# A hybrid decoder step: two DeltaNet heads beside each other, and a lane of its own for the last attention pair

## The chip, the cores and the metric

The kernel runs on one NeuronCore of a Trainium2 chip. The core has engines that run side by side, each with its own in-order instruction stream: TensorE (PE, matrix products; its weight loads are shown as PEld), VectorE (DVE), ScalarE (ACT), GpSimd (POOL) and SyncE (SP, which here issues the transfers). The metric is the device time of one execution in microseconds. The kernel before was timed in three runs.

## The reference

The reference is one inference step of a two-layer decoder trunk. A prompt of 2048 tokens with 16 learned tokens ahead of it, and 8 decode sequences of one token each, pass through both layers. Width is 1024, everything is float32.

Layer 0 makes one projection of the normed input and feeds two kinds of heads with it. Eight attention heads (two key and value heads) look at a window of 128 positions. Four gated DeltaNet heads with keys and values of 128 go through a short convolution and then, chunk by chunk, through the delta rule. For each head and chunk:

```python
a_mat = where(strict, (kbeta @ k.T) * decay, 0) + eye
u, w  = triangular_solve(a_mat, [v * beta, kbeta * exp(gc)])
# over the chunks, S carried from one to the next
v_new = u - w @ S
o     = q_dec @ S + qk @ v_new
S     = S * g_last + k_dec.T @ v_new
```

Both results are gated, put side by side and projected out (`w_out_ab`), and added to the input. Layer 1 is linear attention with a data-dependent decay (GLA), four heads with keys of 128 and values of 256, also in chunks, with its own gate and output projection. A last norm makes `y`. The states, the window caches and the last rows of the convolution are outputs too.

## The kernel before, in words

The prompt is cut into 4 groups of 512 tokens, worked through one after the other; group 0 also carries the 16 learned and the 8 decode tokens, so its tiles are 536 columns wide and its projections run in two halves of 268. Activations lie with the channels on the partitions, 8 tiles of 128 channels. Every float32 operand of a large projection is split into a high and a low part; a projection is three products (high by high, high by low, low by high), which appear in the profile as `pp<-t,wh` and `pp<-t,wl` at L110, the line of the helper `MM`. PSUM is split into 4 banks for projections (`pp`) and 4 for everything else (`pc`). In group 0 the weights are split on ACT (`wh<-raw`, L365) and DVE (`wl<-raw`, L113) and written back to memory as parts; later groups load the parts (`wh<-wd`, `wl<-wd`). The weights pass through 8 tiles (`NW`), two for each projection.

A group goes through these stages: `ab_head` (keys, then the convolution of DeltaNet head 0), `ab_rest` (the other three convolutions `c1` to `c3` and the four attention pairs `s0` to `s3`, in the order of the list `ORDER`), `ab_out` (the output projection in two parts, the first over those of the 8 mixed outputs that come first in `OUT_AB`), `c_main` (GLA) and `c_out`. The head of the next group (`ab_head`) stands inside `c_out` of the group before.

Projections are the bulk work and are emitted by `bulk`. Everything else is a generator that yields a planned latency and its planned TensorE time. `spawn` puts a generator into a lane; a lane runs one generator at a time, and the next starts no earlier than the time at which the last one ended. A clock `Clock.pe` counts planned TensorE time; between two pieces of a projection, `bulk` lets every stream step whose time has come:

```python
while streams:
    s = min(streams, key=lambda q: q[0])
    if s[0] > Clock.pe:
        break
    step(s)
```

The tile framework then orders the instructions of each engine from what was emitted and its dependencies.

Tiles are counted by hand. `take` waits for room in bulk code and meanwhile drives the streams on (`advance`); `take_in` does so inside a stream by yielding. `T` is the pool of wide work tiles (52, of which 47 may be taken), `BQ` a pool of four larger tiles: a DeltaNet head needs two (its convolved queries and keys, and its products), a GLA head three (values, queries and keys, output).

A DeltaNet head (`dn_head`) is a chain of 34 steps: transposed keys (L1466), decays, products, the inverse of the triangular matrix by doubling from 32x32 blocks (tiles `inv`, products `pc<-inv,t` and `pc<-inv,inv`), transposed values and queries (L1583, L1591), then for each of 4 chunks three steps with the state, and last a norm and the transposes of the output (L1637). All heads run in the lane `dn`. In group 0 the learned tokens are a chunk of their own in the lane `dnx` and the decode tokens a stream in the lane `smp`.

An attention pair (`swa_pair`) works on one head of each key and value group: scores (products `pc<-kh,t`), softmax, transposes (L1015) and values (`pc<-t,va`), for 4 blocks, and then splits its output with the last subtraction on GpSimd (`store_m`). All pairs run in the lane `swa`. The last pair of `ORDER`, u = 3, has a form of its own with shorter steps. In the GLA stage a head (`gla_head`) multiplies masked products (`AMK`), values (`VH`), scaled keys and the states (`Tg`, `SM`), and its output `On` is transposed at L1812.

Of the kernel before, what the change touches and what calls it, by code (L numbers as in the profile page):

```python
# [21 lines left out]
META = 16  # L22
EX = SMP + META
NT, NT_FREE = 52, 5
NW = 8
AHEAD = 8
W_AHEAD = 1
RS_AT = 5

ORDER = "c1 s0 c2 s1 c3 s2 s3".split()  # L30

# [38 lines left out]
def kernel(ctx: ExitStack, tc: tile.TileContext, ins, outs):  # L70
# [12 lines left out]
    def nm(s):  # L83
        cnt[0] += 1
        return f"{s}_{cnt[0]}"
# [9 lines left out]
        return ft(dt)  # L95

    def t512(shape=(128, 128), dt=F32):
        return wk.tile(list(shape), dt, tag="t512", bufs=4, name=nm("t5"))

    def sm(shape=(128, 32), dt=F32):  # L100
        return wk.tile(list(shape), dt, tag="sm", bufs=20, name=nm("sm"))

    def cb(shape=(128, 512)):
        return pc.tile(list(shape), F32, tag="pc", name=nm("pc"))
# [287 lines left out]
    def step(s):  # L392
        try:
            lat, pe = next(s[1])
            s[0] += lat
            Clock.pe += pe
        except StopIteration:
            s[2] = False
            streams.remove(s)
            lanes[s[3]].pop(0)  # L400
            if lanes[s[3]]:
                n = lanes[s[3]][0]
                n[0] = max(n[0], s[0])
                streams.append(n)

    def bulk(gen, hooks=()):

        for i, c in enumerate(gen):
# [3 lines left out]
            while streams:  # L412
# [2 lines left out]
                    break  # L415
                step(s)

    def join(ss):
        while any(s[2] for s in ss):
            advance()  # L420


    live = {"BQ": 0, "T": 0}
    caps = {"BQ": 4, "T": NT - NT_FREE}

    def room(tag, n=1):
        return live[tag] + n <= caps[tag]
# [15 lines left out]
        live[tag] -= n  # L443

    def until(cond):
        while not cond():
            yield 0.5, 0.0

    def take_in(tag, n=1):
        yield from until(lambda: room(tag, n))  # L450
# [213 lines left out]
    def new_group(g):  # L664
        q = Grp()
        q.g = g
        q.C = CMAX if g == 0 else 512
        q.off = EX if g == 0 else 0
        q.halves = [(0, q.C // 2), (q.C // 2, q.C // 2)] if g == 0 else [(0, 512)]
        q.x0 = 0 if g == 0 else EX + 512 * g  # L670
        q.wins = [(b, q.off + 128 * b) for b in range(4)]
        q.seq0 = SMP if g == 0 else 0
        q.s0 = 1 if g == 0 else 0
        q.nscan = 4 + q.s0
        q.layer = "AB"
        q.M = [[None] * 8, [None] * 8]
        q.can_m = False
        q.dn = []
        q.sw = []
        return q  # L680

# [211 lines left out]
    def ab_conv(q, h):  # L893
        g = q.g
        take("BQ", 2)
        CQ = wk.tile([128, 2, CMAX - SMP], F32, tag="BQ", bufs=4, name=nm("CQ"))
        take("T", 2)
        CV = ft(shape=(128, CMAX - SMP))
        G_, vdone, done = [], [], []

        first, got = [], []

        def meta():
            yield from take_in("T")
            got.append(1)
            yield from dn_head(q, h, CQ, CV, 0, 1, 32, 0, G_, SMP, META, vdone, done, first)

        def chunks():
            if g == 0:
                yield from until(lambda: got)  # L910
            else:
                first.append(1)
            yield from take_in("T", 2)
            yield from dn_head(q, h, CQ, CV, META if g == 0 else 0, 4, 128, q.s0, G_, q.off, 128, vdone, done, first)
            give("BQ")
            give("T")
        for j in range(3):
            ct = 3 * h + j
            Tt = ft()

            def w(i):
                return PV[:, P_CW + 4 * ct + i:P_CW + 4 * ct + i + 1]

            def ev_c(ps, c0, n):

                m = n - q.seq0
                if g == 0:
                    A.copy(XS[:, ct, :], ps[:, 0:SMP])
                    R = ps[:, SMP - 3:n]
                    V.memset(R[:, 0:3], 0.0)  # L930
                else:
                    R = ft()
# [12 lines left out]
            if j == 1:  # L945
                if g == 0:
                    q.dn.append(spawn(meta(), "dnx", 0.5, tag=h))
                s = spawn(chunks(), "dn", LAT["dn_spawn"], tag=h)
                q.dn.append(s)
        vdone.append(1)  # L950
        G_.append(ft())
        bulk(ab_proj(q, 21 + h, gate(q, G_[0], 4 + h)))
        done.append(1)
        if g == 0:
            q.dn.append(spawn(dn_sample(q, h), "smp", tag=h))

    def ab_swa(q, u):
        g, off = q.g, q.off
        take("T", 3)
        QS = [ft(F32R, (128, 512)) for _ in range(2)]  # L960

        def ev_q(ps, c0, n):
            s = 0
            if g == 0:
                for kv in range(2):
                    A.activation(QX[:, 4 * kv + u, :], ps[64 * kv:64 * kv + 64, 0:EX], AF.Copy, scale=0.125)
                s = EX
            m = n - s
            for kv in range(2):
                r = slice(64 * kv, 64 * kv + 64)  # L970
                o = slice(64 - 64 * kv, 128 - 64 * kv)
                A.activation(QS[kv][r, 0:m], ps[r, s:n], AF.Copy, scale=0.125)
                STT(QS[kv][o, 0:m], ps[r, s:n], 0.125, QS[kv][r, 0:m].bitcast(F32), mul, sub)
        bulk(ab_proj(q, 1 + u, ev_q))
        gx = []
        if g == 0 and len(q.sw) == 3:
            q.xs = [spawn(swa_extra(q, gx), "sx", LAT["sx_0"])]
        Gt = ft()
        bulk(ab_proj(q, 5 + u, gate(q, Gt, u)))
        gx.append(1)  # L980
        return spawn(swa_pair(q, u, QS, Gt), "swa", LAT["sw_spawn"])

    def swa_pair(q, u, QS, Gt):
        g, off = q.g, q.off
# [141 lines left out]
    def c_v(q, h):  # L1126
        g, s0 = q.g, q.s0
        take("BQ")
        VH = wk.tile([128, 4, 256], F32, tag="BQ", bufs=4, name=nm("VH"))
        if h == 0:  # L1130
            gkp = cb()
            gkx = cb() if g == 0 else None
# [31 lines left out]
    def c_logs(q):  # L1164

        C = q.C
        yield from take_in("T", 4)
        yield from take_in("BQ", 2)
        q.mn, Bs = [], []
        for p in range(2):  # L1170
            B = wk.tile([128, 2, CMAX], F32, tag="BQ", bufs=4, name=nm("Bc"))
            for h in (2 * p, 2 * p + 1):
                mn = ft()
                bg = PV[:, P_BGK + h:P_BGK + h + 1]
                for (c0, n) in q.halves:
                    ps = cb()
                    MM(ps[:, :n], WU[:, 128 * h:128 * h + 128], GS[:, c0:c0 + n])
                    A.activation(B[:, h % 2, c0:c0 + n], ps[:, :n], AF.Abs, bias=bg)
                    TS(mn[:, c0:c0 + n], ps[:, :n], bg, 0.0, add, amin)
                q.mn.append(mn)  # L1180
                yield LAT["dec_1"], 0.25
            A.activation(B[:, :, :C], B[:, :, :C], AF.Exp, scale=-1.0)
            Bs.append(B)
# [71 lines left out]
    def c_head(q, h, nxt):  # L1255
# [8 lines left out]
        join([q.dec])  # L1264
        E = q.E
        take("BQ", 2)
        QKt = wk.tile([128, 2, CMAX], F32, tag="BQ", bufs=4, name=nm("QKt"))
        for j in range(2):
            def ev_m(ps, c0, n):
                TT(QKt[:, j, c0:c0 + n], ps, E[j][:, c0:c0 + n], mul)  # L1270
# [165 lines left out]
    def dn_head(q, h, CQ, CV, q0, nch, L, s0, G_, mc0, nv, vdone, done, first):  # L1436
# [47 lines left out]
            A.activation(DT[R_, c, 0:L], Rp[R_, c, 0:L], AF.Exp, bias=SC["ng"][R_, s0 + c, h:h + 1])  # L1484
        yield LAT["dn_R"], 0.45 * pe
        if L == 128:
            BQ = wk.tile([128, 4, 2, 128], F32, tag="BQ", bufs=4, name=nm("BQ"))
        else:
            BQ = ftt((128, 1, 64)).rearrange("p c (x l) -> p c x l", x=2)
        for c0 in range(0, nch, 2):  # L1490
# [18 lines left out]


        yield LAT["dn_at"], 0.45 * pe
        tc4 = lambda: wk.tile([128, 4, 32], F32, tag="inv", bufs=6, name=nm("inv"))

        P1, Y, X = tc4(), tc4(), tc4()
        for a in range(nb):
# [60 lines left out]
            A.copy(YF[0:64, :, 64:128], pi[0:64, 1])  # L1576
            yield 0.0, 0.4

        while not vdone:
            yield 0.5, 0.0  # L1580
        vT = cb((128, 4, 128))
        for c in range(nch):
            T.transpose(vT[R_, c], blk(2, c), ident)  # L1583
# [46 lines left out]
        on = O  # L1630
        TT(on[R_, 0:nch], O[R_, 0:nch], bc(st2[R_, 3, 0:nch], 128), mul)
        yield LAT["dn_n"], 0.0
        while not (done and q.can_m):
            yield 0.5, 0.0
        oT = cb((128, 4, 128))
        for c in range(nch):
            T.transpose(oT[:, c, 0:L], on[R_, c], ident[R_, 0:L])  # L1637
# [129 lines left out]
    def gla_head(qq, h, QKt, VH, ce, Gz, done):  # L1767
# [14 lines left out]
        A.copy(KT, kT)  # L1782
        yield LAT["gl_t"], 1.4
        st = sm((128, 4, 4))
        On = wk.tile([128, 4, 256], F32, tag="BQ", bufs=4, name=nm("On"))
        QS = ft(shape=(128, 4, 128))
        TT(QS, QKt[:, 0, off:off + 512].rearrange("p (c t) -> p c t", c=4), bc(ce[:, s0:s0 + 4], 128), mul)
        for c0 in (0, 2):
# [31 lines left out]

    def gla_sample(q, h, QKt, VS, ea, Gz):
        vrow = rows_of(VS[0:8], 256)
        QZ = wk.tile([128, 72], F32, tag="t512", bufs=4, name=nm("QZ"))
        V.memset(QZ, 0.0)
        V.tensor_copy(QZ.rearrange("p (b x) -> p x b", x=9)[:, 0, :], QKt[:, 0, 0:SMP])
        o = cb()
# [155 lines left out]
```

## Time and profile before

| what | value |
|---|---|
| median of 3 runs | 2223.55 us (2215.16 to 2228.36) |
| profiled execution, its own time | 2217.27 us |
| its span, first to last instruction | 2215.5 us |
| PE busy | 2146.0 us (97%), 17290 matmuls |
| PEld busy | 1805.4 us (81%) |
| DVE busy | 1216.4 us (55%) |
| ACT busy | 833.4 us (38%) |
| POOL busy | 263.1 us (12%) |
| granted TensorE clock, mean | 0.988 |
| moved by DMA | 400.17 MB, mean 181 GB/s |

A row of the timeline gives start, duration, engine, line, operation, output<-input with buffer numbers left out, shapes, count, and in brackets the idle time before it with what ended it. Matmuls are pipelined and their ends are modelled, so the time from one start to the next tells more than a duration. A row of the waits names who waited for whom, the total, the number of times and the longest. A row by stage gives a stretch in microseconds from the start of the span, its length and the busy time of each engine in it, the granted clock as a share of full speed, the busy share of the DMA engines and what they moved.

### The profile page before, as it was taken

How to read it: one execution, taken by the hardware profiler on the slowest of the kernel's cores; microseconds unless marked ns; L12 is line 12 of the kernel's file. 1: busy time of each engine (PE TensorE's matmuls, PEld its weight loads, DVE VectorE, ACT ScalarE, POOL GpSimd, SP SyncE). 2: the span in 40 equal slices, each digit the busy share in tenths (PEclk: the TensorE clock that was granted, in tenths of full speed). 3: DMA queues.
4: the chain of work that ended last, by engine and by line, in shares of the span. 5: the costliest groups of instructions: out<-in, count | busy, mean ns of one | idle time of the engine just before them, and what ended most of it. 6: DMA issues, size and time to landing. Idle time of an engine off the chain costs nothing.

```text
span 2215.5 us, 43744 instructions
## 1 busy us (share of the span) xinstructions
PE 2146.0 (97%) x17290; PEld 1805.4 (81%) x17290; DVE 1216.4 (55%) x3501; ACT 833.4 (38%) x2235; POOL 263.1 (12%) x314
## 2 busy tenths in 40 slices
PE   8889999999999999999999999999999999999997
PEld 7878888888879777788887777778887877778886
DVE  7778876654564566544344466545344466545323
ACT  5445544443352244343232244334333244334222
POOL 0011100021210011002220011002130000001111
PEclk9999999999999999999999999999999999999999
DMA  6643537767767623474555823454554743364444
GB/s 237 206 161 125 194 121 245 249 219 262 254 205 246 241 97 103 136 242 149 177 203 164 275 98 115 143 202 170 177 183 148 243 168 104 102 239 159 164 147 153
DMA packets 162623, 400.17 MB, mean 181 GB/s; under 512 B 22049, under 2 KB 54465, under 8 KB 162385
## 3 DMA queue, kind: packets, MB, share of 16 engines
q1 hardware_dynamic: 162416, 397.37, 52.7%
q8 instruction: 136, 2.23, 0.4%
q14 instruction: 71, 0.57, 0.1%
HBM read 297.19 MB, written 101.70 MB: 180 GB/s over the span
## 4 chain that ended last, share of the span: by engine, by line
PE 70%; DMA 3%; DVE 3%; ACT 2%; issue 2%; POOL 1%; SPq 0%; DVEq 0%; POOLq 0%; ACTq 0%
PE pp L110 53%; PE pc L110 14%; DVE t L116 1%; PE pc L1015 1%; DMA wl<-wd 1%; DMA raw<-in_w_co 1%; DMA t<-in_xT 1%; PE pc L1812 1%; DVE t L113 1%; POOL sm L206 0%; POOL t L113 0%; ACT t L1004 0%; PE pc L1583 0%; PE pc L1466 0%; PE pc L1591 0%
## 5 line engine op out<-in xcount | busy, mean ns | idle before, releaser
L110 PE MATMUL pp<-t,wh 128*128 128x512 f32 (+1 forms) x4528 | 1260.3, 363 | 17.6 <-ACT t L150 7.8
L110 PEld LDWEIGHTS pp<-t,wh 128*128 128x128 f32 x4528 | 783.1, 190 | 127.8 <-issue 17.4
L110 PE MATMUL pp<-t,wl 128*128 128x512 f32 (+1 forms) x2264 | 809.2, 358 | 6.3 <-DMA wl<-wd 5.2
L110 PEld LDWEIGHTS pp<-t,wl 128*128 128x128 f32 x2264 | 429.5, 190 | 67.0 <-DMA wl<-wd 6.5
L113 POOL TENSOR_TENSOR t<-t,t 128x512 fp32r<-128x512 f32 (+3 forms) x128 | 163.6, 1295 | 580.9 <-ACT t L660 345.5
L110 PE MATMUL pp<-wh,t 128*128 128x256 f32 (+1 forms) x1088 | 209.6, 288 | 2.9 <-DVE QKt L113 2.9
L116 DVE SCALAR_TENSOR_TENSOR t<-t,PV,t 128x512 f32<-128x512 f32 (+4 forms) x232 | 172.6, 754 | 55.7 <-ACT t L935 23.2
L110 PEld LDWEIGHTS pp<-wh,t 128*128 128x128 f32 x1088 | 172.7, 191 | 5.0 <-DVE QKt L113 3.1
L116 DVE SCALAR_TENSOR_TENSOR t<-pp,t 128x512 f32<-128x512 f32 (+3 forms) x160 | 92.8, 585 | 128.0 <-PE pp L110 78.5
L206 POOL TENSOR_TENSOR sm<-sm,mh 128x2 f32<-128x2 f32 (+3 forms) x84 | 68.0, 809 | 772.5 <-DVE sm L116 320.1
L110 PE MATMUL pp<-wl,t 128*128 128x256 f32 (+1 forms) x544 | 155.3, 286 | 0.0
L113 DVE TENSOR_TENSOR wl<-raw,wh 128x512 fp32r<-128x512 f32 (+3 forms) x138 | 91.5, 680 | 24.2 <-ACT wh L365 12.8
L110 PEld LDWEIGHTS pp<-wl,t 128*128 128x128 f32 x544 | 103.6, 191 | 0.7
L365 ACT CAST wh<-raw 128x512 fp32r<-128x512 f32 (+2 forms) x122 | 68.2, 587 | 61.2 <-DMA raw<-in_w_c 17.9
L113 DVE TENSOR_TENSOR t<-t,t 128x512 f32<-128x512 f32 (+4 forms) x103 | 62.9, 614 | 42.4 <-ACT t L489 41.2
L1004 ACT ACTIVATE t<-t,sm 128x257 f32<-128x257 f32 x128 | 64.1, 503 | 56.8 <-DVE sm L116 56.6
L113 DVE TENSOR_TENSOR QKt<-pp,t 128x512 f32<-128x512 f32 (+1 forms) x40 | 23.3, 586 | 112.1 <-PE pp L110 106.5
L110 PEld LDWEIGHTS pc<-t,t 128*128 128x128 f32 (+4 forms) x496 | 63.7, 165 | 22.4 <-ACT t L1609 3.8
L110 PE MATMUL pc<-t,t 128*128 128x128 f32 (+5 forms) x496 | 79.4, 270 | 1.7 <-PE pc L110 0.7
L489 ACT ACTIVATE t<-t 128x512 f32<-128x512 f32 (+1 forms) x70 | 44.1, 631 | 96.5 <-DVE t L116 66.7
L113 DVE TENSOR_TENSOR t<-pp,t 128x268 f32<-128x268 f32 (+1 forms) x90 | 44.3, 497 | 49.6 <-PE pp L110 36.0
L1017 ACT COPY t<-pc 128x512 f32<-128x512 f32 x64 | 37.4, 584 | 63.7 <-PE pc L1015 63.3
(334 smaller groups left out, 2788.4 us busy)
## 6 DMA issues: line engine op xcount, KB each, us to landing
wh<-wd SPq DMA_DIRECT2D x157, 512.0 KB, 3.7
wl<-wd SPq DMA_DIRECT2D x157, 512.0 KB, 4.6
wd<-wh SPq DMA_DIRECT2D x55, 512.0 KB, 3.5
wd<-wl SPq DMA_DIRECT2D x55, 512.0 KB, 5.1
t<-in_xT SPq DMA_DIRECT2D x72, 256.0 KB, 4.9
raw<-in_w_ab SPq DMA_DIRECT2D x25, 512.0 KB, 5.2
raw<-in_w_c SPq DMA_DIRECT2D x16, 512.0 KB, 4.7
out_yp<-t SPq DMA_DIRECT2D x32, 256.0 KB, 2.9
```

The lines of the kernel that those rows point to most:

```text
L110: T.matmul(out, lhsT, rhs, start=start, stop=stop)
L113: return (eng or V).tensor_tensor(out, a, b, op=op)
L116: V.scalar_tensor_tensor(out, a, s, b, op0=op0, op1=op1)
L206: G.tensor_tensor(out, x, mh[0:x.shape[0]].to_broadcast(list(x.shape)), op=ALU.pow)
L365: last[0] = A.copy(hi[:, c], raw[:, c])
L489: A.activation(sq[:, :q.C], x, AF.Square)
L1004: A.activation(S_[:, kv], S_[:, kv], AF.Exp, bias=st[:, 2 + kv:3 + kv], accum_out=st[:, 4 + kv:5 + kv])
L1015: T.transpose(pt[:, kv, x], S_[:, kv, 128 * x:128 * x + 128], ident)
L1017: A.copy(PT, pt)
L1812: T.transpose(oT[:, c], On[:, c, 128 * j:128 * j + 128], ident)
```

## The change

`ab_conv` no longer puts a head's chunk stream into the lane `dn`. It makes the entry by hand, with a time before which it may not start, and appends it to a list of the group. With head 0 it spawns one stream `together` in the lane `dn`, which works through that list. At most `DN_RUN` = 2 heads run in it, and a head is taken up when the one before has made at least `DN_OFF` = 12 steps. In every round each running head makes one step. The round's latency is the larger of the two, times `PAIR_LAT` = 1.25 when both made a step. `DN_HOLD` adds to a head's earliest time: nothing in group 0, and in the later groups 50 for head 0 and 25 for head 2. A wait inside a stream now yields no latency (`None`), which `step` takes as 0.5 and `together` does not count as a step.

The last attention pair of `ORDER` is spawned into a lane of its own (`swaTrue`), the other three share one (`swaFalse`).

The pools grow: `BQ` from 4 to 6 tiles, also for the GLA stage, `t512` from 4 to 8, `sm` from 20 to 24, `inv` from 6 to 10. The scratch for dynamic DMA is set to 1024.

```diff
+NBQ = 6
...
+PAIR_LAT, DN_OFF, DN_RUN = 1.25, 12, 2
+DN_HOLD = ((0, 0, 0, 0), (50, 0, 25, 0))
...
-        return wk.tile(list(shape), dt, tag="t512", bufs=4, name=nm("t5"))
+        return wk.tile(list(shape), dt, tag="t512", bufs=8, name=nm("t5"))
...
-        return wk.tile(list(shape), dt, tag="sm", bufs=20, name=nm("sm"))
+        return wk.tile(list(shape), dt, tag="sm", bufs=24, name=nm("sm"))
...
-            s[0] += lat
+            s[0] += 0.5 if lat is None else lat
...
+    def together(gens):
+        run, left = [], 4
+        while left:
+            if gens and gens[0][1] <= Clock.pe and len(run) < DN_RUN and (not run or run[-1][1] >= DN_OFF):
+                run.append([gens.pop(0), 0])
+            lat, pe = [], 0.0
+            for a in list(run):
+                r = next(a[0][0], False)
+                if not r:
+                    a[0][2] = False
+                    run.remove(a)
+                    left -= 1
+                elif r[0] is not None:
+                    a[1] += 1
+                    lat.append(r[0])
+                    pe += r[1]
+            yield (max(lat) * (PAIR_LAT if len(lat) > 1 else 1.0) if lat else None), pe
...
-    caps = {"BQ": 4, "T": NT - NT_FREE}
+    caps = {"BQ": NBQ, "T": NT - NT_FREE}
...
     def until(cond):
         while not cond():
-            yield 0.5, 0.0
+            yield None, 0.0
...
-                s = spawn(chunks(), "dn", LAT["dn_spawn"], tag=h)
+                s = [chunks(), Clock.pe + LAT["dn_spawn"] + DN_HOLD[g > 0][h], True, "dn", h]
                 q.dn.append(s)
+                q.pair.append(s)
+                if h == 0:
+                    spawn(together(q.pair), "dn", LAT["dn_spawn"])
...
-        return spawn(swa_pair(q, u, QS, Gt), "swa", LAT["sw_spawn"])
+        return spawn(swa_pair(q, u, QS, Gt), "swa" + str(u == int(ORDER[-1][1])), LAT["sw_spawn"])
...
-        tc4 = lambda: wk.tile([128, 4, 32], F32, tag="inv", bufs=6, name=nm("inv"))
+        tc4 = lambda: wk.tile([128, 4, 32], F32, tag="inv", bufs=10, name=nm("inv"))
...
-    nc = _bacc.Bacc("TRN2", target_bir_lowering=False, num_devices=1)
+    nc = _bacc.Bacc("TRN2", target_bir_lowering=False, num_devices=1, dynamic_dma_scratch_size=1024)
```

The other `BQ` allocations take `bufs=NBQ` as well, and two waits in `dn_head` that yielded 0.5 now use `until`.

More of the change, by code (lines that the diff above doesn't have):

```diff
@@ L678, in new_group @@
         q.dn = []
+        q.pair = []
         q.sw = []
@@ L895, in ab_conv @@
         take("BQ", 2)
-        CQ = wk.tile([128, 2, CMAX - SMP], F32, tag="BQ", bufs=4, name=nm("CQ"))
+        CQ = wk.tile([128, 2, CMAX - SMP], F32, tag="BQ", bufs=NBQ, name=nm("CQ"))
         take("T", 2)
@@ L1128, in c_v @@
         take("BQ")
-        VH = wk.tile([128, 4, 256], F32, tag="BQ", bufs=4, name=nm("VH"))
+        VH = wk.tile([128, 4, 256], F32, tag="BQ", bufs=NBQ, name=nm("VH"))
         if h == 0:
@@ L1170, in c_logs @@
         for p in range(2):
-            B = wk.tile([128, 2, CMAX], F32, tag="BQ", bufs=4, name=nm("Bc"))
+            B = wk.tile([128, 2, CMAX], F32, tag="BQ", bufs=NBQ, name=nm("Bc"))
             for h in (2 * p, 2 * p + 1):
@@ L1266, in c_head @@
         take("BQ", 2)
-        QKt = wk.tile([128, 2, CMAX], F32, tag="BQ", bufs=4, name=nm("QKt"))
+        QKt = wk.tile([128, 2, CMAX], F32, tag="BQ", bufs=NBQ, name=nm("QKt"))
         for j in range(2):
@@ L1486, in dn_head @@
         if L == 128:
-            BQ = wk.tile([128, 4, 2, 128], F32, tag="BQ", bufs=4, name=nm("BQ"))
+            BQ = wk.tile([128, 4, 2, 128], F32, tag="BQ", bufs=NBQ, name=nm("BQ"))
         else:
@@ L1577, in dn_head @@
             yield 0.0, 0.4
-        while not vdone:
-            yield 0.5, 0.0
+        yield from until(lambda: vdone)
         vT = cb((128, 4, 128))
@@ L1632, in dn_head @@
         yield LAT["dn_n"], 0.0
-        while not (done and q.can_m):
-            yield 0.5, 0.0
+        yield from until(lambda: done and q.can_m)
         oT = cb((128, 4, 128))
@@ L1784, in gla_head @@
         st = sm((128, 4, 4))
-        On = wk.tile([128, 4, 256], F32, tag="BQ", bufs=4, name=nm("On"))
+        On = wk.tile([128, 4, 256], F32, tag="BQ", bufs=NBQ, name=nm("On"))
         QS = ft(shape=(128, 4, 128))
@@ L1822, in gla_sample @@
         vrow = rows_of(VS[0:8], 256)
-        QZ = wk.tile([128, 72], F32, tag="t512", bufs=4, name=nm("QZ"))
+        QZ = wk.tile([128, 72], F32, tag="t512", bufs=8, name=nm("QZ"))
         V.memset(QZ, 0.0)
```

## The prediction

> **What bounds the kernel now.** I read the page first, then the busy time by stage, then what TensorE waits for, then the order of time around the places where it waits.
>
> ```profile
> span 2215.5 us, 43744 instructions
> PE 2146.0 (97%) x17290; PEld 1805.4 (81%) x17290; DVE 1216.4 (55%) x3501; ACT 833.4 (38%) x2235; POOL 263.1 (12%) x314
> q1 hardware_dynamic: 162416, 397.37, 52.7%
> ```
>
> TensorE is busy for 2146.0 of 2215.5 us: 69.5 us are idle. The change keeps all 17290 matmuls, so it can win only idle time, the cost of changing between kinds of matmul, and time at a lowered clock. Where these lie (columns: stretch, length, then PE, PEld, DVE, ACT, POOL busy with counts, granted clock, DMA share, GB/s):
>
> ```profile
> 53.30:72.00 18.70, 12.69 (x245) 9.98 (x243) 13.57 (x56) 4.79 (x19) 1.75 (x3) 0.73 0.14 53
> 134.00:147.00 13.00, 7.09 (x45) 5.95 (x43) 8.72 (x33) 7.44 (x24) 2.16 (x3) 0.74 0.34 94
> 311.00:346.00 35.00, 29.10 (x206) 25.98 (x204) 24.96 (x119) 11.44 (x35) 2.58 (x2) 0.85 0.52 158
> 388.00:570.00 182.00, 169.76 (x1221) 154.42 (x1219) 101.21 (x270) 75.68 (x170) 25.16 (x22) 0.98 0.69 238
> 730.00:941.00 211.00, 210.35 (x1980) 161.87 (x1979) 126.45 (x402) 81.15 (x251) 18.43 (x30) 1.00 0.42 139
> ```
>
> The last row is the stage the change is about, in group 1: DeltaNet heads 1 to 3 and all local attention run there, and TensorE idles for 0.65 of 211 us. Groups 2 and 3 look the same. The idle time is in group 0: 6.0, 5.9 and 5.9 us in the first three rows (DeltaNet and attention) and 12.2 us in the fourth (GLA). There the clock falls too:
>
> ```profile
> 61.60:71.90 10.30, 7.73 (x214) 6.72 (x215) 7.03 (x27) 0.00 (x0) 0.00 (x0) 0.50 0.11 41
> 140.10:147.00 6.90, 3.07 (x13) 2.96 (x13) 5.71 (x17) 4.13 (x12) 1.07 (x1) 0.51 0.64 178
> 327.90:338.10 10.20, 10.20 (x50) 9.17 (x49) 4.54 (x24) 1.20 (x4) 1.29 (x1) 0.50 0.45 153
> 437.00:440.50 3.50, 3.50 (x18) 3.50 (x18) 3.50 (x14) 0.00 (x0) 0.54 (x1) 0.51 0.49 199
> 546.30:549.70 3.40, 3.40 (x11) 3.04 (x12) 1.39 (x4) 1.93 (x4) 0.00 (x0) 0.50 0.83 281
> ```
>
> Work at clock 0.5 takes twice as long, so half of the busy time in these five is lost: 3.9 + 1.5 + 5.1 + 1.75 + 1.7 = 13.9 us. In the later groups one thing is left, the end of the attention stage (waits between 900 and 2000 us; total, times, longest):
>
> ```profile
> PE pp L110 <- DMA wl<-wd: 5.2, 3, 2.0
> PE pp L110 <- POOL t L113: 1.0, 3, 0.3
> ```
>
> That is 6.2 us, once in each of groups 1 to 3. All that the change can reach is therefore 6.2 + (6.0 + 5.9 + 5.9 + 12.2) + 13.9 = 50.1 us.
>
> **The change part by part.** *Own lane for the last attention pair.* In group 1:
>
> ```profile
> 917.61 0.66 PE L110 MATMUL pc<-t,va 128*64 128x128 f32 x8
> ...
> 923.87 0.64 PE L110 MATMUL pc<-kh,t 128*128 128x256 f32 x4
> ...
> 938.88 0.66 PE L110 MATMUL pc<-t,va 128*64 128x128 f32 x8
> ...
> 941.95 0.50 PE L110 MATMUL pp<-t,wh 128*128 128x512 f32 x1 [0.34 <-POOL t L113]
> ...
> 949.06 0.50 PE L110 MATMUL pp<-t,wl 128*128 128x512 f32 x1 [1.76 <-DMA wl<-wd]
> ```
>
> The pair before (u=2) does its last values product at 917.61. Its last step stands 4.5 + 1.0 planned units (sw_p, and the last yield) ahead of the lane's next entry, which makes 923.1: pair u=3 begins at 923.87, so the lane did hold it. It ends at 938.88, its product is split on GpSimd, and only then do the four open sums of the output projection get their last term (0.34 us). They hold eight weight tiles, all that there are (NW = 8), so the next weights come late: 1.76 us. With a lane of its own the pair would start after its spawn, but it also needs 6 tiles T of 47: 17 are held by the layer's input, 10 by five finished outputs, 8 by DeltaNet head 3, 9 by pair u=2 and 3 by itself, 47 in all. So it starts when head 3 ends.
>
> ```profile
> L1466 PE MATMUL pc<-CC,CQ x16: 270/272/329, 651.6 to 854.1; 128*128 128x128 f32 x16
> L1637 PE MATMUL pc<-CC,t x16: 270/272/273, 723.5 to 904.6; 128*128 128x128 f32 x16
> ```
>
> These are the first and last products of heads in group 1: head 0 runs from 651.6 to 723.5, head 3 from 854.1 to 904.6. Head 2 is held for 25 units; if that moves it by 17 of them, to 814, it is 40 units into the 48 that the planned latencies of a head add up to when head 3 comes. Some six rounds are then shared, at the larger of two latencies times 1.25, 18 units where head 3 alone needs 8: head 3 ends 5 to 10 us later, at 910 to 914, and the pair starts some 9 us or more ahead of 923.87. That brings its end ahead of the open sums. Bounds: 0 (it waits for tiles until 923 anyway) to 6.2 us. I take 4.
>
> *Two heads in one stream.* In groups 1 to 3 the heads are spread by when their convolutions are emitted:
>
> ```profile
> 740.98 0.63 PE L1466 MATMUL pc<-CC,CQ 128*128 128x128 f32 x4
> ...
> 797.14 0.60 PE L1466 MATMUL pc<-CC,CQ 128*128 128x128 f32 x4
> ```
>
> Head 1 starts at 740.98, 17 us after head 0 ended: it waits for its convolution, not for head 0. The hold of 50 units moves head 0 from 651.6 to about 701, its end beside the start of head 1. Head 2 moves from 797.14 by at most its 25, so to 797 to 822. Their matmuls go from a stretch where TensorE is full to another one that is full. What a merged round saves can be seen where two bursts already met:
>
> ```profile
> 757.89 0.45 PE L110 MATMUL pc<-inv,t 32*32 32x32 f32 x32
> 758.27 0.73 PE L110 MATMUL pp<-t,wh 128*128 128x512 f32 x2
> 758.84 0.39 PE L110 MATMUL pp<-t,wl 128*128 128x512 f32 x1
> ...
> 863.31 0.45 PE L110 MATMUL pc<-inv,t 32*32 32x32 f32 x32 [0.22 <-DVE inv L113]
> 863.69 0.66 PE L110 MATMUL pc<-t,va 128*64 128x128 f32 x8
> 864.28 0.73 PE L110 MATMUL pp<-t,wh 128*128 128x512 f32 x2
> 864.85 0.40 PE L110 MATMUL pp<-t,wl 128*128 128x512 f32 x1
> ...
> 910.00 0.63 PE L110 MATMUL pp<-t,wh 128*128 128x512 f32 x2
> 910.46 0.39 PE L110 MATMUL pp<-t,wl 128*128 128x512 f32 x1
> ```
>
> The burst of 32 small products takes 0.38 us from start to start, alone (757.89) and in front of another burst (863.31). The two wide matmuls behind a burst take 0.57 us in both places, where two in a plain stream take 0.46 (910.00): leaving a burst costs 0.11 us, and I estimate as much for entering one. A merge saves one entry and one exit, 0.22 us, and the one shown met a wait of 0.22. With some 15 shared rounds in each of four groups the bounds are 13 us won (0.22 × 60) and 13 us lost. The row that shows a merge has the two cancel; I take 0.
>
> In group 0 nothing is held, a head can start beside the one before, and DVE carries more at once. The pool there is 17.8 us idle (first three rows of the stages) and 10.5 us of lowered clock. The first of these, at 53 to 72, comes while head 0 is alone and stays. The third, at the end of the stage, has the last pair and the extra tokens in it; a pair that starts earlier fills part of it. The bounds are 11 us won (5.9 + 5.1 of the third) and the slow rival's loss; I take 3 won, a quarter.
>
> *Six BQ tiles.* In the GLA stage a head takes three (values, queries and keys, output). With four, the next head's projections are emitted only after the head before is driven to its end, with no projection between its steps. Group 0 shows such steps (waits from 388 to 570 us):
>
> ```profile
> PE pc L110 <- ACT t L1782: 2.0, 1, 2.0
> PE pc L110 <- DVE Tg L116: 1.9, 2, 1.6
> PE pc L110 <- DVE AMK L1777: 1.8, 2, 1.3
> PE pc L1812 <- ACT On L1804: 1.6, 2, 1.0
> ```
>
> 7.3 us, and 1.7 of clock behind them (546.3 row). With six a second head fits. Bounds: 0 to 9.0 us; I take 5.
>
> *The rest.* More t512, sm and inv tiles only lift limits. By their sizes in the code they take 13 KB in a partition, for which the diff lowers the scratch for dynamic DMA; the queue that moved the data is a hardware one (q1 above), so I cost that at nothing, and if it were wrong every load would show it. No instruction and no DMA is added.
>
> *The clock.* The window at 327.9 stands at 0.50 though the longest idle near it is 1.67 us:
>
> ```profile
> 326.24 0.24 PE L616 MATMUL pc<-CC,t 64*128 64x64 f32 x1 [1.67 <-DVE t L120]
> ```
>
> The Trainium skill, "TensorE: Matmul & The Clock Gate", on HAM oscillation, has a gate that falls behind idle gaps of more than some 3.4 us. By that rule only the 5.9 us gap would pay, the pool would be 12.4 us smaller, and the sum by shares some 3 us less; the trace does not agree here.
>
> *Sum.* 4 + 0 + 3 + 5 = 12 us off a span of 2215.5. The profiled execution took 2217.27 us, so 2205.3 by its own time; the median of the runs, 2223.55, stands 6.3 above it, and in those terms I predict 2211.5.
>
> **The rivals.** *Nothing is gained.* The pair waits for its tiles, as counted above, and GLA is bound by its own chain of steps. For it: 0.65 us idle in the stage meant. Against: the count of BQ tiles in the code is what drives the GLA steps together. Result 2219.5 to 2227.5, about 2223.5.
>
> *Group 0 opens up.* With more buffers three fifths of the 50.1 us go, 30 us: 2193.5. For it: idle and lowered clock come together, one removed removes the other. Against: the first row's stall precedes every second head.
>
> *Slower: splits of weights stand behind two heads.* In group 0 ACT and DVE also split the weights. Waits from 134 to 147 us:
>
> ```profile
> PE pp L110 <- DVE t L113: 5.9, 1, 5.9
> ACT t L1708 <- DVE t L1698: 4.7, 1, 4.7
> ```
>
> ACT stood still for 4.7 us at a decode head's step, the splits behind it were late, and TensorE paid 5.9 us and 1.5 of clock, 7.4 us. Two heads in flight put more such steps ahead of splits. One more stall for each of heads 1 to 3 is 22 us; less the 4 of the lane, 18 more: 2241.5. It decides from the second such stall on (15 against my 12). Against: a head starts only when its convolution is through, which keeps the overlap short.
> The Trainium skill, "TensorE: Matmul & The Clock Gate", says in its architectural detail that ScalarE and VectorE are strict first in, first out; the 4.7 us row agrees.
>
> **How the numbers follow.** My forecast has 0.48, within 2203 to 2220; nothing gained 0.18; group 0 open 0.18; slower 0.16. A measurement of this kernel tells about 0.5%, 11 us, from no change. The forecast lies at that line: 0.26 beyond, 0.22 within. Faster is 0.26 + 0.17 = 0.43, same 0.22 + 0.18 + 0.01 = 0.41, slower 0.16. The range goes from 2190, the case of group 0 and some, to 2236, up to the second stall: it leaves out most of the slow case.
>
> **What would show it.** Right: no wait for wl at the end of the attention stage in groups 1 to 3; pair u=3 starting before u=2 ends; the four GLA waits of group 0 gone; bursts of 32 still 0.38 us. Wrong: the first kh product of the last pair still some 5 us behind the last values product of the one before; new waits on splits between 72 and 311 us; the stage of 211 us longer than its matmuls.

## The result, and the profile after

| | before | after |
|---|---|---|
| median of 5 runs each | 2219.39 us (2215.16 to 2228.36) | 2202.05 us (2200.07 to 2205.61) |
| ratio of the two | | 0.9918, 95% interval 0.9898 to 0.9938 |
| profiled execution, its own time | 2217.27 us | 2200.07 us |

The kernel became 0.8% faster, and the whole interval lies beyond the 0.5% line. The two profiled executions differ by 17.2 us; the prediction's sum was 12. The page of after:

```profile
span 2197.9 us, 43736 instructions
PE 2136.8 (97%) x17290; PEld 1814.4 (83%) x17290; DVE 1222.6 (56%) x3501; ACT 835.3 (38%) x2235; POOL 261.7 (12%) x314
```

The matmuls are the same 17290, and PE is busy 9.2 us less (2146.0 before). So 9 of the 17 us are not idle time. To see where they went, both traces were cut at the same work: group 0's attention stage runs from the 1st to the 1600th product of the projections (`pp`), its GLA stage to the 2880th, and groups 1 to 3 from there to the 8000th. What comes behind that takes 188.7 us before and 189.0 after, and is left out below. Before:

```profile
7.80:380.10 372.30, 348.59 (x3693) 314.64 (x3694) 286.96 (x1023) 175.96 (x543) 33.52 (x45) 0.96 0.53 180
380.10:604.50 224.40, 212.16 (x1542) 192.84 (x1541) 124.57 (x320) 91.32 (x204) 39.29 (x33) 0.98 0.72 252
604.50:2026.80 1422.30, 1408.53 (x11068) 1143.99 (x11067) 735.78 (x1994) 515.41 (x1361) 158.20 (x199) 1.00 0.51 173
```

After:

```profile
7.90:374.40 366.50, 344.94 (x3693) 312.25 (x3694) 288.19 (x1023) 176.68 (x544) 33.58 (x45) 0.97 0.54 182
374.40:592.30 217.90, 209.74 (x1541) 192.27 (x1540) 124.58 (x320) 90.80 (x204) 38.84 (x33) 0.98 0.74 260
592.30:2008.90 1416.60, 1404.99 (x11069) 1155.69 (x11068) 740.89 (x1995) 517.10 (x1361) 157.06 (x199) 1.00 0.52 174
```

The counts agree within one, so each pair of rows holds the same matmuls. The stages gave 5.8, 6.5 and 5.7 us, so two thirds of the gain lie in group 0. Length less PE busy is idle time; half of the busy time inside the stretches granted 0.50 is lost to the clock (worked out from the trace's clock records); the rest is work at full clock:

| us, before to after | group 0 attention | group 0 GLA | groups 1 to 3 | sum |
|---|---|---|---|---|
| idle | 23.7 to 21.6 | 12.2 to 8.2 | 13.8 to 11.6 | −8.4 |
| lost to the clock | 12.2 to 9.1 | 3.4 to 2.7 | 1.7 to 0 | −5.5 |
| work at full clock | 336.4 to 335.9 | 208.7 to 207.0 | 1406.8 to 1405.0 | −4.1 |

Inside group 0 the stretches that the prediction showed read after:

```profile
53.30:72.00 18.70, 12.68 (x252) 9.97 (x251) 12.46 (x53) 5.31 (x22) 1.74 (x3) 0.78 0.08 31
134.00:147.00 13.00, 11.81 (x264) 10.50 (x264) 9.42 (x36) 6.78 (x23) 2.57 (x4) 1.00 0.14 22
311.00:346.00 35.00, 31.17 (x265) 27.44 (x266) 31.89 (x155) 17.97 (x55) 2.64 (x2) 1.00 0.59 177
```

The first stall is as it was (6.0 us idle). In the second, 5.9 us idle became 1.2 and the clock rose from 0.74 to 1.00; in the third, 5.9 became 3.8 and 0.85 became 1.00.

In group 1 the last attention pair now ends at 918.71 instead of 938.88 (12.2 of these 20.2 us had been won before the group began), and TensorE's waits from 900 to 2000 us name no `wl` any more:

```profile
918.71 0.66 PE L114 MATMUL pc<-t,va 128*64 128x128 f32 x8
```

```profile
PE pc L114 <- DVE t L117: 2.7, 3, 2.2
PE pc L114 <- DVE inv L124: 1.4, 2, 0.9
PE pc L114 <- DVE t L120: 1.4, 2, 0.7
PE pc L114 <- issue: 1.0, 1, 1.0
```

The 5.2 us behind `wl<-wd` are gone, but waits on DVE, which were there before too, have grown. Over the whole stretch of groups 1 to 3 (to the 8000th product) the waits on DVE that the view lists add up to 8.7 us instead of 5.4. That is why the idle time of groups 1 to 3 fell by 2.2 us only.

### The profile page after: what moved, and what is told of

It reads as the page before. It is cut to its first block, busy times and chain, and to the rows that moved or that the text cites. A ratio compares the mean times of both kernels' runs of the same rounds, so it can differ in the third digit from the quotient of the medians.

```text
span 2197.9 us, 43736 instructions
## 1 busy us (share of the span) xinstructions
PE 2136.8 (97%) x17290; PEld 1814.4 (83%) x17290; DVE 1222.6 (56%) x3501; ACT 835.3 (38%) x2235; POOL 261.7 (12%) x314
## 4 chain that ended last, share of the span: by engine, by line
PE 60%; DMA 4%; DVE 3%; issue 1%; ACT 1%; POOL 0%; SPq 0%; DVEq 0%; POOLq 0%; ACTq 0%
PE pp L114 44%; PE pc L114 13%; DMA t<-x1d 4%; DVE t L120 1%; PE pc L1044 1%; DVE t L117 1%; DVE inv L117 1%; DMA t<-x2d 1%; PE pc L1839 0%; ACT junk L1497 0%; SPq L1364 0%; PE pc L1807 0%; PE pc L1664 0%; PE pc L1611 0%; DVE BQ L117 0%
## 5 line engine op out<-in xcount | busy, mean ns | idle before, releaser
L117 DVE TENSOR_TENSOR wl<-raw,wh 128x512 fp32r<-128x512 f32 (+3 forms) x138 | 93.7, 694 | 25.4 <-ACT wh L369 13.8
```

What stands on the lines that cost most here:

```text
L117: return (eng or V).tensor_tensor(out, a, b, op=op)
```

## The experiments

The theory was that of the prediction: the lane frees the weights at the end of the stage, the BQ tiles open GLA, and the pairs do little. Its rivals put the gain on the pairs or on the tiles instead. Each ratio is to the kernel before, timed beside it on the same chip, with its 95% interval.

**The lane alone** (on the kernel before).

```diff
-        return spawn(swa_pair(q, u, QS, Gt), "swa", LAT["sw_spawn"])
+        return spawn(swa_pair(q, u, QS, Gt), "swa" + str(u == int(ORDER[-1][1])), LAT["sw_spawn"])
```

> The kernel before with nothing changed but the lane: the last attention pair has its own. Theory A (the lane takes away the wait at the end of the attention stage, the buffers loosen GLA, the pairing itself gives nothing): the wait of the output projection for wl goes from 5.2 us in groups 1 to 3 to under 1.5, and the time falls by 2 to 5 us, ratio 0.998 to 0.999. Theory B (the two heads beside each other are what gains): ratio 1.000, the wait for wl stays above 3 us, since the pair still waits for its tiles.

Measured: 2204.06 us, ratio 0.9932 (0.9914 to 0.995), some 15 us. One line of the change gives nearly all of it, several times what the prediction had for the lane. In the cut by stages:

```profile
7.50:377.90 370.40, 347.64 (x3693) 313.75 (x3694) 285.91 (x1023) 176.40 (x544) 33.80 (x45) 0.96 0.54 180
377.90:600.60 222.70, 214.21 (x1540) 195.20 (x1540) 123.69 (x320) 91.15 (x204) 39.87 (x33) 0.97 0.74 256
600.60:2011.60 1411.00, 1404.30 (x11069) 1144.66 (x11068) 736.90 (x1995) 515.49 (x1361) 158.44 (x199) 1.00 0.52 174
```

Groups 1 to 3 are 11.3 us shorter: idle 6.7 instead of 13.8 us (7.1), work 2.5 and clock 1.7. That is 5.6 us more than the whole change wins there. No wait for `wl` is left between 900 and 2000 us. The two stages of group 0 are 1.9 and 1.7 us shorter: 4.7 us less idle (1.0 in attention, 3.7 in GLA) and 1.9 less work, but 3.0 more lost to the clock. The order of time in group 1:

```profile
905.98 0.64 PE L110 MATMUL pc<-kh,t 128*128 128x256 f32 x4
...
912.85 1.09 PE L110 MATMUL pc<-t,va 128*64 128x128 f32 x16
...
927.68 0.66 PE L110 MATMUL pc<-t,va 128*64 128x128 f32 x8
```

The pair's first scores come at 905.98 and not at 923.87, some 6 us behind head 3 (its output transposes stand at 899.5) and ahead of the last values product of the pair before, which is the first half of the burst at 912.85. The pair ends 11.2 us earlier, 3.9 of which had been won before the group began.

**The pool sizes alone** (on the kernel before; six BQ tiles, in the planner's count too; `sm` and the scratch as changed, not shown here).

```diff
-        return wk.tile(list(shape), dt, tag="t512", bufs=4, name=nm("t5"))
+        return wk.tile(list(shape), dt, tag="t512", bufs=8, name=nm("t5"))
...
-    caps = {"BQ": 4, "T": NT - NT_FREE}
+    caps = {"BQ": 6, "T": NT - NT_FREE}
...
-        tc4 = lambda: wk.tile([128, 4, 32], F32, tag="inv", bufs=6, name=nm("inv"))
+        tc4 = lambda: wk.tile([128, 4, 32], F32, tag="inv", bufs=10, name=nm("inv"))
```

> The kernel before with nothing changed but the pool sizes of the change (BQ 6, t512 8, sm 24, inv 10, small scratch); heads one after the other, pairs in one lane. Theory A: the stage of GLA in group 0 loses the four waits on AMK, Tg, On and the scaled keys (7.3 us) and gains about 5 us, the rest of group 0 moves by a few us, in all 2209 to 2214 against 2219, ratio 0.9955 to 0.998. Theory B: ratio 0.999 to 1.001.

Measured: 2217.9 us, ratio 0.9987 (0.9976 to 0.9997). The pools alone are worth a tenth of a per cent, and the GLA stage of group 0, where 5 us had been expected, takes 223.8 us against 224.4.

**The changed kernel with the lane undone.**

```diff
-        return spawn(swa_pair(q, u, QS, Gt), "swa" + str(u == int(ORDER[-1][1])), LAT["sw_spawn"])
+        return spawn(swa_pair(q, u, QS, Gt), "swa", LAT["sw_spawn"])
```

> The changed kernel with one part undone: the last pair is back in the lane of the others. Theory A: the wait for wl at the end of the attention stage of groups 1 to 3 is back with 4 to 6 us in all, and the time is 3 to 6 us above the changed kernel's 2202, so 2205 to 2208, ratio 0.9935 to 0.995. Theory B: 2202 to 2203, ratio 0.992.

Measured: 2207.49 us, ratio 0.9955 (0.9936 to 0.9973). Without the lane the rest still wins 0.45%. It stands 5.4 us above the changed kernel's 2202.05 (8 by the two ratios), where the lane alone gave 15: the parts do not add up. Idle time in groups 1 to 3 is 14.6 us here. The wait for `wl`, expected back with 4 to 6 us, is back with 1.1; most of the idle time stands on DVE, with listed waits of 10.3 us.

**Lane and pools, heads one after the other** (both edits above on the kernel before: the changed kernel without its pairs).

> The kernel before with lane and pool sizes of the change, but the four heads still one after the other as before. Theory A: nearly all of the gain, 2203 to 2209, ratio 0.992 to 0.9955. Theory B: at most a third of it, 2213 or more, ratio over 0.997.

Measured: 2201.59 us, ratio 0.9922 (0.9907 to 0.9937), level with the changed kernel. The part that the change is named for has no net worth that can be measured.

**Holds at zero** (on the changed kernel).

```diff
-DN_HOLD = ((0, 0, 0, 0), (50, 0, 25, 0))
+DN_HOLD = ((0, 0, 0, 0), (0, 0, 0, 0))
```

> The changed kernel with the holds taken out: heads 0 and 2 of groups 1 to 3 start as soon as they can. Theory A (the pairing moves work between stretches in which TensorE is full, so its times matter little): 2199 to 2206, ratio 0.991 to 0.994, as the changed kernel. Theory B (the holds are what makes pairs, and pairs gain): 2207 or more, ratio above 0.994, with waits on the tiles inv and on DVE above the changed kernel's.

Measured: 2201.07 us, ratio 0.9911 (0.9891 to 0.9932). The holds change no time that can be measured.

**Six BQ tiles there, but GLA may take four** (on the changed kernel; set at the start of `c_main`, the GLA stage, and back at the start of `c_out`).

```diff
+        caps["BQ"] = 4
...
+        caps["BQ"] = NBQ
```

> The changed kernel with one part undone: in the GLA stage no more than four BQ tiles may be taken, as before; elsewhere six. Theory A (the two further tiles let a second GLA head begin, and end the waits on AMK, Tg and the scaled keys): these waits are back in group 0, the stage from 388 to 570 us loses 4 to 6 us, the time is 2206 to 2209, ratio 0.994 to 0.9955. Theory B (the GLA gain of the trace of the changed kernel is chance): 2202, ratio 0.992.

Measured: 2202.14 us, ratio 0.9917 (0.9894 to 0.994); the GLA stage of group 0 takes 219.7 us against 217.9. What is left between 388 and 575 us:

```profile
PE pp L114 <- DVE QKt L117: 3.7, 1, 3.7
PE pc L114 <- DVE Tg L120: 2.7, 2, 1.5
PE pc L1841 <- ACT On L1833: 1.7, 2, 1.0
```

Of the three waits expected back only `Tg` is, at 2.7 us, and the time does not show it. In the changed kernel (388 to 570 us) it is this:

```profile
PE pp L114 <- DVE QKt L117: 3.8, 1, 3.8
PE pc L1839 <- ACT On L1831: 1.6, 2, 1.0
PE pc L114 <- DVE t L117: 1.5, 1, 1.5
PE pc L114 <- ACT t L1809: 0.5, 1, 0.5
...
PE pc L114 <- DVE Tg L120: 0.3, 1, 0.3
```

With six, `Tg` fell to 0.3 and a wait for `t` of 1.5 us, which the four-tile kernels have at 0.3 or less, came in its place. Both stand at the same kind of product, `pc<-Tg,t` (at 548.45 and 550.51 us in the changed kernel), for its two inputs: first the scaled queries `t`, then the state `Tg`. In the ten traces with six tiles in GLA the wait for `Tg` is 0.3 to 1.4 and that for `t` 1.5 to 2.2 us; in the four with four tiles `Tg` is 1.9 to 2.9.

**Pairs in group 0 only** (on the changed kernel; indentation and the lines taken out are not shown).

```diff
+                if g == 0:
                     s = [chunks(), Clock.pe + LAT["dn_spawn"] + DN_HOLD[g > 0][h], True, "dn", h]
                     q.pair.append(s)
                     if h == 0:
                         spawn(together(q.pair), "dn", LAT["dn_spawn"])
+                else:
+                    s = spawn(chunks(), "dn", LAT["dn_spawn"], tag=h)
```

> The changed kernel, but the heads run beside each other in group 0 alone; in groups 1 to 3 they run one after the other in the lane, without a hold. Theory A (in groups 1 to 3 the pairs only add waits of TensorE on inv and DVE, 0.8 to 3.7 us a group against lane and pools without pairs): 2196 to 2200, ratio 0.9895 to 0.9915. Theory B (pairs gain there too): 2205 or more, ratio above 0.9935.

Measured: 2196.44 us, ratio 0.9889 (0.9868 to 0.9909), the lowest of all.

**Pairs in groups 1 to 3 only** (the same edit with `g > 0`).

> The complement: the changed kernel with pairs in groups 1 to 3 alone, group 0 one after the other. Theory A (what the pairs gain they gain in group 0, where the stall before the third convolution and the lowered clock behind it go): 2205 to 2211, ratio 0.9935 to 0.9965, with the 5.9 us wait near 140 us back. Theory B: 2200 to 2203, ratio 0.9915 to 0.993.

Measured: 2201.91 us, ratio 0.9912 (0.9891 to 0.9933). Expected were 2205 to 2211 if what the pairs gain is gained in group 0; the time does not tell it from the changed kernel. The trace does: between 50 and 358 us group 0's stall behind weight splits is back, and the clock from 134 to 147 us is 0.85 again.

```profile
PE pp L114 <- DVE t L117: 5.9, 1, 5.9
```

**Three versions side by side**: the changed kernel, pairs in group 0 only, and no pairs (lane and pools), timed beside each other; the kernels are those above, unchanged.

> The changed kernel itself, on one chip with the next three, so that they can be compared without the spread between chips. Theory A (pairs gain in group 0 and lose in groups 1 to 3): about 2202, ratio 0.991 to 0.993, between the next two. Theory C (pairs are worth nothing anywhere once lane and pools are there; what differed so far is spread): the three agree within 0.003.

> Pairs in group 0 alone, again, beside the changed kernel. Theory A: 3 to 6 us below it, 2196 to 2199, ratio 0.9885 to 0.9905. Theory C: within 0.003 of it, ratio 0.991 or more.

> Lane and pool sizes of the change without pairs, again, beside the other two. Theory A: 4 to 7 us above pairs in group 0 alone, and within 3 us of the changed kernel, 2200 to 2205, ratio 0.9915 to 0.9935. Theory C: the same as both within 0.003.

| version | median | ratio (95%) | group 0 attention: length, idle, clock | groups 1 to 3: length, idle, clock |
|---|---|---|---|---|
| changed | 2201.0 | 0.9901 (0.9884 to 0.9918) | 363.7, 20.7, 5.7 | 1417.7, 11.7, 1.7 |
| pairs in group 0 only | 2196.31 | 0.9883 (0.9865 to 0.9901) | 363.4, 20.8, 5.5 | 1411.1, 6.8, 0 |
| no pairs | 2200.91 | 0.9904 (0.9887 to 0.992) | 368.6, 21.5, 10.6 | 1409.9, 5.6, 0 |

The rows behind the last two columns, and the stretch from 134 to 147 us; first the version with pairs in group 0 only:

```profile
8.20:371.60 363.40, 342.58 (x3692) 309.77 (x3693) 288.04 (x1023) 176.81 (x544) 33.57 (x45) 0.98 0.54 184
...
591.70:2002.80 1411.10, 1404.35 (x11069) 1144.19 (x11068) 737.58 (x1995) 515.23 (x1361) 158.72 (x199) 1.00 0.51 174
...
134.00:147.00 13.00, 11.81 (x291) 10.41 (x289) 9.22 (x35) 6.65 (x22) 2.88 (x4) 1.00 0.21 69
```

Then the one without pairs:

```profile
7.40:376.00 368.60, 347.07 (x3692) 313.38 (x3693) 286.12 (x1023) 176.53 (x544) 33.82 (x45) 0.96 0.54 181
...
597.70:2007.60 1409.90, 1404.35 (x11068) 1144.13 (x11067) 737.27 (x1995) 515.37 (x1361) 158.23 (x199) 1.00 0.51 175
...
134.00:147.00 13.00, 7.10 (x50) 6.10 (x49) 7.64 (x30) 7.29 (x24) 2.16 (x3) 0.83 0.24 69
```

And the changed kernel in groups 1 to 3:

```profile
591.30:2009.00 1417.70, 1406.04 (x11068) 1156.74 (x11067) 741.21 (x1994) 517.72 (x1361) 156.73 (x199) 1.00 0.51 174
```

The traces show two effects of opposite sign. In group 0 pairs take away the stall at 134 to 147: in all eight traces with pairs there PE is busy for 11.81 of the 13 us at a clock of 1.00, in the six without for 7.09 to 7.10 at 0.74 to 0.90. The idle time of the whole stage hardly changes (20.8 and 21.5: shorter waits on DVE come in, up to 2.3 us more on `t` behind the transposes of the attention pairs and 1.1 on `inv`), but the time lost to the clock is 5.5 to 10.2 us in the eight and 10.5 to 14.1 in the six, and the stage takes 363.4 to 367.4 us against 368.6 to 374.9. In groups 1 to 3 pairs add idle time: 9.7 to 12.5 us in the six traces with pairs there and the lane, 5.6 to 10.2 in the five with the lane and no pairs there; here it is 11.7 against 5.6, and the weight loads are busy for 12.6 us more (1156.74 against 1144.13). Together the two give nothing.

The times bear this out only in part. By the intervals the three medians are not told apart, and they lie within the 0.003 that the other expectation allowed; the version with the gain and without the loss was 4.6 to 4.7 us lower here, and the lowest where it ran before. But if the two effects simply added up, pairs in groups 1 to 3 only would be the slowest version, some 5 us above the one without pairs. Its ratio is 0.9912, that of no pairs 0.9922 and 0.9904. So a loss by pairs in groups 1 to 3 is seen in the time only next to pairs in group 0, and why it isn't seen without them stays open.

**Four BQ tiles in the changed kernel.**

```diff
-NBQ = 6
+NBQ = 4
```

> The changed kernel with the pool BQ at four tiles instead of six, its limit and its tiles; the other pools as changed. If the two further tiles, and not their count in the planner, loosen the GLA stage of group 0: the waits on AMK, Tg and the scaled keys come back there, the time is 3 to 6 us above the changed kernel, 2205 to 2208, ratio 0.9935 to 0.995; heads also meet less, since a third convolution must wait. If the smaller pools (t512, sm) loosen it: 2200 to 2204, ratio 0.991 to 0.993, and these waits stay as in the changed kernel.

Measured: 2204.43 us, ratio 0.9923 (0.9904 to 0.9942), 3.4 us above the changed kernel timed beside it, with intervals that overlap. Its GLA stage of group 0 takes 220.1 us, that of the changed kernel beside it 220.2. So whatever the 3.4 are, they are not in the stage that the tiles were credited with. TensorE's waits of this kernel there (374 to 594 us):

```profile
PE pc L114 <- DVE Tg L120: 2.0, 2, 1.5
...
PE pc L114 <- DVE t L117: 0.2, 1, 0.2
```

`Tg` 2.0 and `t` 0.2 with four tiles, 0.3 and 1.5 with six: the same exchange as above. Of the other waits expected back, `AMK` is at 0.2 and the scaled keys (`t` from ACT) at 1.4 us.

## Why the prediction was right, and where not

**The direction, the range and the mechanism named first held.** The forecast was 12 us off, 17 came, and "faster", at 0.43 the largest chance, is what happened. The rivals did not happen: no weight split stands behind two heads (the 5.9 us wait went away instead of multiplying), and group 0 opened by a part only (12.3 us, where that rival had most of 30).

That the sum came within 5 us is in part luck. The lane was taken 11 us too small, a loss of the pairs of some 6 us was missed, and the pools were taken 2 to 3 too large; these errors nearly cancel.

**The mis-sized step is the lane: taken at 4, bounded at 6.2, measured alone at some 15.** Three things were left out of that bound. First, the share within the bound was too small: of 6.2 us of idle time the lane alone won all and a little more (7.1). With the lane alone the pair starts 6 us behind head 3, which fits the count of tiles T, and that was early enough. In the changed kernel it does not wait for the end of head 3: its first scores stand at 899.01, ahead of head 3's output transposes and of the last values product of the pair before (the first half of the burst at 906.68).

```profile
899.01 0.71 PE L114 MATMUL pc<-kh,t 128*128 128x256 f32 x4
...
906.12 0.63 PE L1664 MATMUL pc<-CC,t 128*128 128x128 f32 x4 [0.31 <-DVE sm L1034]
906.68 1.09 PE L114 MATMUL pc<-t,va 128*64 128x128 f32 x16
```

So there the step "it starts when head 3 ends" fails, though the end that it was to explain came. Second, a bound from idle time cannot hold what is not idle: 2.5 us of matmul work and 1.7 of clock went too. How much of these is due to the lane one execution does not tell: the work at full clock of groups 1 to 3 lies between 1404.0 and 1406.8 us in the fourteen traces, and before is the highest. Third, the pair has its own lane in group 0 also. The stretch from 311 to 346 us was booked under the two heads, "a pair that starts earlier fills part of it"; the lane alone starts it earlier, at 324.54 instead of 338.86 (first row before, second with the lane alone):

```profile
338.86 0.52 PE L110 MATMUL pc<-kh,t 128*128 128x256 f32 x3
```

```profile
324.54 0.74 PE L110 MATMUL pc<-kh,t 128*128 128x256 f32 x4
```

With it the idle time of the stretch falls from 5.9 to 4.3 us, and in this execution the clock goes from 0.85 to 1.00:

```profile
311.00:346.00 35.00, 30.66 (x261) 26.63 (x259) 28.14 (x144) 16.41 (x55) 3.83 (x3) 1.00 0.50 150
```

The clock is no sure gain of the lane: lane and pools without pairs had the stretch at 0.80 in one execution and at 1.00 in the other. And with the lane alone what was won there in clock was lost elsewhere in the stage: 12.0 us lost as a whole, 12.2 before.

**Two heads in one stream: 0 from merges held, +3 in group 0 was near, a loss in the later groups was missed.** The heads do run beside each other, for longer than estimated: in group 1 head 1 makes its first products at 721.2 and head 0 its output transposes at 761.3, so 40 of some 70 us are shared. A merge in the changed kernel:

```profile
739.81 0.45 PE L114 MATMUL pc<-inv,t 32*32 32x32 f32 x32
740.19 0.71 PE L114 MATMUL pc<-S,CQ 128*128 128x128 f32 x4
740.66 0.47 PE L114 MATMUL pp<-t,wh 128*128 128x512 f32 x1
```

The 32 small products still take 0.38 us from start to start, and the burst behind them 0.47. Where such bursts stand in an unbroken stream of projections, what they add to it is, in the median, 1029 ns for 32 small and 4 wide products merged, and 585 + 450 = 1035 ns apart, so a merge saves nothing; work at full clock in groups 1 to 3 is 1405.0 us with pairs and 1404.35 without. Group 0 won some 5, from a stall that the prediction had put down as the slow rival's seed: it expected pairs to add such stalls, and they removed this one, together with its clock. In groups 1 to 3 nothing was idle in the attention stage (0.65 of 211 us), and the prediction read this as "the pairs have nothing to win" but not as "they can only lose": with pairs TensorE waits more. It cost some 6 us of idle time in the versions side by side (11.7 against 5.6), some 4 in the mean of all traces with the lane (11.5 against 7.3), within the bound of 13. The waits are on DVE: over groups 1 to 3 those that the view lists add up to 7.0 to 10.3 us in the seven traces with pairs there, and to 2.7 to 5.4 in the seven without. The likely reason is that two heads' steps stand behind one another on DVE; no run changed DVE's order alone, so that part is argued and not shown.

**The six BQ tiles: taken at 5, worth about nothing in their stage.** The four waits fell as predicted, from 7.3 to 2.4 us (`On` 1.6, `t` from ACT 0.5, `Tg` 0.3, `AMK` none), but a wait for another `t`, 1.5 to 2.2 us in the six-tile kernels, took their place. The prediction asked which waits go and not what is late next. The stage did become 6.5 us shorter; it nearly did so with four tiles too (220.1 and 219.7 us against 224.4 before, both with pairs), six tiles with the pools alone left it at 223.8, and its idle time is 7.8 to 10.4 us in every version run here against 12.2 before, with the lane alone 8.5. Why that stage differs in before stays open: there is one trace of before, and between two executions of one kernel the stage differed by 6 us (215.4 and 221.7).

**The rest**, memory for the pools and the lower scratch, cost nothing, as said: the pools alone stand at 0.9987. The stall at 53 to 72 stayed, as said. The holds, expected only to shift heads within full stretches, changed no time that can be measured (0.9911 without them, 0.9918 with).

In short: the sum was 4 + 0 + 3 + 5. By the runs it is some 15 for the lane, +5 and some −6 for the pairs as the traces have it, and 2 to 3 for all pools together (0.9987 of 2219.57 us), where 5 stood for the BQ tiles alone. Since the parts do not simply add up, these are sizes of each part where it was run, and not shares of the 17.

## What to carry to other kernels

When a change has several parts, cost each part in every stage that it touches: here the one-line part acted in all four groups and was booked in three. A stage in which the bound engine is never idle has nothing to give to a rearrangement but something to lose, so put the rearrangement only where there is idle time; here that is group 0, and pairs there alone gave 2196.3 us, the lowest median of all versions, though by less than the intervals tell. A wait that goes is a gain only if another in the same chain isn't already due: `Tg` went and `t` came.

## What the runs showed of the hardware

The place where the clock falls is no fixed property of the kernel. Lane and pools without pairs was profiled twice. The first execution (span 2203.4 us) and the second (2195.7 us), with three of the stretches that were at 0.50 in one of them:

```profile
328.10:341.80 13.70, 13.70 (x67) 12.00 (x67) 5.89 (x33) 3.19 (x10) 1.30 (x1) 0.50 0.12 34
754.80:758.20 3.40, 3.40 (x62) 2.27 (x48) 0.89 (x3) 0.00 (x0) 0.00 (x0) 0.50 1.01 400
```

```profile
328.10:341.80 13.70, 13.12 (x111) 11.48 (x111) 10.56 (x53) 5.51 (x18) 1.52 (x1) 1.00 0.41 127
552.20:562.40 10.20, 9.52 (x36) 8.33 (x35) 3.40 (x10) 4.97 (x17) 2.37 (x3) 0.50 0.53 153
```

The same code, the same matmuls, and the low stretch lies at 328 in one and at 552 in the other. Nor does it need one long idle gap: the stretch at 754.8 is busy throughout, and the gap just ahead of it is 1.57 us; in the changed kernel the stretch from 64.0 to 74.2 (longest idle gap 1.66 us) is at 0.50:

```profile
64.00:74.20 10.20, 8.09 (x216) 7.07 (x217) 6.94 (x25) 0.00 (x0) 0.00 (x0) 0.50 0.15 51
```

The Trainium skill, "TensorE: Matmul & The Clock Gate", on HAM oscillation, gives as its rule no idle gap of TensorE above some 3.4 us; these rows do not agree that keeping to it is enough. Several short gaps close together may count as well: of the 3.4 us just ahead TensorE was busy for 0.50 in the changed kernel and for 1.83 ahead of 754.8. But with the pools alone it was busy for 2.84 of the 3.4 us ahead of a half-clock stretch at 397.7, so no threshold can be read from these runs. For reading one trace against another it means that a gain of 5 us in clock, of one execution each, is no evidence by itself. What carries it here is the count: the stretch from 134 to 147 us at 1.00 in eight traces of eight with pairs in group 0, and below 0.91 in six of six without.
